# Down projection: the second block's weights loaded piece by piece, and its first row loads issued by GpSimd

## The chip, the cores and the metric

The kernel runs on one core of one Trainium2 chip. The metric is the device time of one execution in microseconds (us); lower is better. The time before is the median of three timed runs. The profile is one more execution, taken by the hardware profiler; its span runs from the first to the last instruction on the core. The engines are called PE (TensorE, the matmuls; its weight loads are shown apart as PEld), DVE (VectorE), ACT (ScalarE), POOL (GpSimd) and SP (SyncE, which here only issues DMAs).

## The reference

The block takes x (1024 tokens by 1024 channels, float32) and computes a dilated attention and a retention side by side, gates and merges them, projects, adds the input, and then runs a channel mixer. Only the end of that mixer is touched here:

```python
xn2 = rmsnorm(x, norm2_g[l])
x = x + jnp.square(jax.nn.relu(xn2 @ w_up[l])) @ w_down[l]
```

`w_up` is 1024 by 4096 and `w_down` is 4096 by 1024, so the hidden matrix h = relu(xn2 @ w_up) squared is 1024 by 4096.

## The kernel before, in words

**Numbers in two parts.** Every matmul operand is held as a high part and a low part (suffix h and l), made by `split` (lines 353 to 357): ACT copies the value into the high part (line 354) and DVE subtracts that from the value to get the low part (line 357). A product is then three matmuls, high by high, high by low and low by high. All matmuls are issued from line 257.

**Seven products for eight.** Large matmuls use Strassen's scheme with seven products called N1 to N7 on sums of quarter blocks. The up projection does so over 16 units (`strassen_order`), each a slice of 256 hidden columns. Its results are turned into the seven operands of the down projection, split (tile `hs`), and stored by SP to `h_d` in DRAM (line 1243).

**The down projection.** `h_d` is read back by rows. The down projection has 8 chunks c of 512 hidden columns and 4 row tiles t in each, 32 units u = 4c + t in all. One unit has seven products of six matmuls each. `load_rows(u)` (lines 1252 to 1260) reads the rows of one unit in two DMAs of 896 KB, `xh` and `xl`, both issued by SP at line 1259. There are three row buffers, taken in turn; they are the up projection's operand tiles (`OP7["N1"]`, `["N5"]`, `["N3"]`), so the first three row loads wait for the last up products that read them, and `load_rows(u + 3)` stands after unit u and waits for its last matmul. `down(u, name)` does one product. In the loop at the end, a pass for u does N6 and N5 of u, N1 of u + 1, N7 of u, N2 of u + 1, N3 and N4 of u; so a unit's rows are first read in the third product of the pass before its own. N1 and N2 of unit 0 are done among the last up products.

**What PE waits for inside a unit.** N1 goes into an accumulator of its own; ACT copies it, negated, into the accumulator of N6, N7 and N4 (line 1279, tile `ms`), and N2 is then added on top of N1, so N2 waits for that copy. The results of N2, N6, N5 and N4 are copied to `Y` by ACT in chunk 0 (line 1286) and added to `Y` by DVE afterwards (line 1288); N7 and N3 are added by DVE. N7 goes on top of N6 and so waits for N6's copy.

**The weights.** The class `Weights` keeps a list of loads and a list of steps for the whole kernel. A chunk of the down projection has four loads of 512 KB (`raw`, issued by SP at line 210, into four buffers used in turn) and seven steps in the order N1, N2, N3, N5, N7, N6, N4. A step splits one piece; those of N5, N7, N6 and N4 first take a sum or difference of two raw tiles on DVE (line 186). A step may go when the earlier piece in its buffer is done with (`free`, called after the last use) and all four loads of its chunk have been issued. `pump` issues all steps that may go, and after each as many loads as there are free raw buffers. Chunks with even c and with odd c have separate buffers; the odd set (`y1a` to `y1c`, 3, `w1a` to `w1c`) lies where up-projection tiles were, and comes free when the up projection is over.

**What sets the order.** Only PE runs in the order of the code (`manual_schedule`). On the other engines a planner orders the instructions: whichever it reckons ready goes first, and of several the one that stands earlier in the code. `tc.keep_in_program_order(i)` forbids it to put i ahead of the instruction that the code issued just before it on that engine; instructions that come later in the code may still pass it. Once the order is planned it is fixed: each engine, and SP with its DMAs, goes through its instructions strictly one after another, and an instruction whose wait is not over holds up all behind it.

Of the kernel before, what the change touches and what calls it, by code (L numbers as in the profile page):

```python
# [10 lines left out]
F = mybir.dt.float32  # L11
# [26 lines left out]
class Weights:  # L38
# [9 lines left out]
    RAW = 3  # L48
    A, B, C, D = (0, 1), (2, 3), 5, 4

    def __init__(self, nc, rawp, wp, split):
        self.nc, self.rawp, self.wp, self.split = nc, rawp, wp, split
        self.raw, self.used, self.next = [], set(), 0
        self.src, self.steps = [], []
        self.place, self.more, self.most = [], None, None
        self.last = {}
        self.units, self.done = {}, set()
        self.plain = self.taken = 0
        self.cycle, self.turn = tuple(range(self.WB)), 0

        self.places = {}

    def claim(self, buf, key):

# [105 lines left out]
    def add_chunks(self, tag, srcs, buffers):  # L170


        for c, quarters in enumerate(srcs):
            base = len(self.src)
            self.place += [(base + i) % (self.RAW + 1) for i in range(4)]
            self.src += quarters
            x00, x10, x11, x01 = range(base, base + 4)
            for name, r, other, op, ends in (
                    ("N1", x00, None, None, ()), ("N2", x10, None, None, ()), ("N3", x11, None, None, ()),
                    ("N5", x00, x01, OP.subtract, ()), ("N7", x01, x11, OP.subtract, (x01,)),  # L180
                    ("N6", x11, x00, OP.add, (x00,)), ("N4", x10, x11, OP.subtract, (x10, x11))):
                buf, key = buffers[c % 2][name], (tag, c, name)

                def step(r=r, other=other, op=op, ends=ends, buf=buf, key=key):
                    if other is not None:
                        self.nc.vector.tensor_tensor(self.raw[r], self.raw[r], self.raw[other], op=op)
                    h, l = self.buffer(buf)
                    self.split(h, l, self.raw[r])
                    self.units[key] = h, l
                    self.used.update(ends)  # L190

                self.steps.append((self.claim(buf, key), x01, step))
# [5 lines left out]

    def load(self):
        n = len(self.raw)  # L200
        if n >= len(self.src):
            return False
        b = self.place[n]
        if any(self.place[m] == b and m not in self.used for m in range(max(0, n - 16), n)):
            return False
        from_ = self.rawp if b < self.RAW else self.more if b == self.RAW else self.most
        if from_ is None:
            return False
        raw = from_.tile([P, UW], F, name=f"raw{b}", bufs=1)
        self.nc.sync.dma_start(raw[:, :self.src[n].shape[1]], self.src[n])  # L210
        self.raw.append(raw)
        return True
# [22 lines left out]

    def free(self, *ids):
        self.done.update(ids)
        self.pump()


class Pipe:
# [48 lines left out]
def strassen_order(units):  # L290


    order = [(0, "N1"), (1, "N1"), (0, "N2"), (1, "N2")]
    for j in range(units):
        late = j + 3 >= units
        order += [(j, "N6"), (j, "N5")] + ([] if late else [(j + 2, "N1")]) + [(j, "N7")]
        order += [(j, "N3")]
        order += [(j + 2, "N2")] if not late else [(units - 1, ("N1", "N2")[j + 3 - units])] if j + 1 < units else []
        order += [(j, "N4")]
    return order  # L300
# [3 lines left out]
def hybrid_block(ctx: ExitStack, tc: tile.TileContext, a: dict, out: bass.AP):  # L304
    nc = tc.nc
# [6 lines left out]
    rawp = pool(ctx, "rawp", 1)  # L312
    wp = pool(ctx, "wp", 1)
# [19 lines left out]
    h_d = dram.tile([FF // 512, 2, 4, P, 7, 2, P], F, name="h_d")  # L333
# [40 lines left out]
        return (slice(0, 512), slice(512, 1024))  # L374


    W = Weights(nc, rawp, wp, split)
    heads = [(slot, g) for slot in range(SLOTS) for g in (1, 2, 0)]
    for u in range(4):
        W.add(a["w_av"][u])  # L380
# [136 lines left out]
    with ExitStack() as ph:  # L517
# [96 lines left out]
        for n, t in enumerate(TILES):  # L614
# [4 lines left out]
            for k in range(KT):  # L619
                wh, wl = W[us[k // 2]]  # L620
                o = (k % 2) * 512
                xs = x01[t] if k < 4 and t >= 4 else [x[:, :, cut(t)] for x in XS[k // 4, t // 4]]
                terms.append((*(x[:, k % 4] for x in xs), wh[:, o:o + 512], wl[:, o:o + 512]))
            ends = {2 * i + 1: (lambda i=i: W.free(us[i])) for i in range(4)} if n == NT - 1 else None
            pipe.step(pm, terms, ends)
            c = px.tile([P, 512], F, name="c", bufs=1)
# [487 lines left out]
    with ExitStack() as ph:  # L1114
# [41 lines left out]
        def load_rows(n):  # L1156

            nb, t = order[n]
            ts = slice(t * P, (t + 1) * P)
            xt = pn.tile([P, 512], F, name="xr")  # L1160
            nc.sync.dma_start(xt, a["x"][ts, halves()[nb]])
            y0 = None
            if nb == 1:
                y0 = pn.tile([P, 512], F, name="y0")
                nc.sync.dma_start(y0, out[ts, :512])
            ahead.append((xt, y0))
# [34 lines left out]
    with ExitStack() as ph:  # L1201
# [50 lines left out]
        def load_rows(u):  # L1252

            if u < len(units):
                c, t = units[u]
                rows[u] = []
                for i, x in enumerate(OP7[("N1", "N5", "N3")[u % 3]]):
                    x = x.rearrange("p a b -> p (a b)")[:, :7 * 2 * P]
                    nc.sync.dma_start(x.bitcast(F), h_d[c, i, t].rearrange("p o k q -> p (o k q)"))
                    rows[u].append(x.rearrange("p (o k q) -> p o k q", o=7, k=2))  # L1260

        def down(u, name):
# [28 lines left out]
            if t == 3:  # L1291
                W.free(("dn", c, name))

        for j, name in strassen_order(NU):
            product("up", j, name, unit, OP7, temps, result)
            if j == NU - 1:
                if name == "N1":
                    load_rows(0)
                if name == "N2":
                    parts = [x.rearrange("p a b -> p (a b)") for x in OP7[name]]  # L1300
                    for i, part in enumerate("ab"):
                        W.places["n2" + part] = [x[:, 1024 * i:1024 * i + 1024] for x in parts]
                    W.free(("place", "n2"))
                if name == "N5":
                    load_rows(1)
                if name == "N7":
                    down(0, "N1")
                if name == "N3":
                    load_rows(2)
                    down(0, "N2")  # L1310
# [3 lines left out]
        Y.update({r: y1.tile([P, D], F, name=f"Y{r}") for t in (1, 3, 2) for r in (t, t + 4)})  # L1314
        for x in "abc":
            W.places["y1" + x] = [y1.tile([P, UW], R, name=f"y1{x}{i}") for i in "hl"]
        W.free(("place", "y1"))


    with ExitStack() as ph:  # L1320
        w1 = pool(ph, "w1", 1)
        for x in "abc":
            W.places["w1" + x] = [w1.tile([P, UW], R, name=f"w1{x}{i}") for i in "hl"]
        W.free(("place", "w1"))
        for u in range(len(units)):
            for name, later in (("N6", False), ("N5", False), ("N1", True), ("N7", False), ("N2", True),
                                ("N3", False), ("N4", False)):
                if u + later < len(units):
                    down(u + later, name)
            load_rows(u + 3)  # L1330
    sumst.close()


# [106 lines left out]
```

## Time and profile before

| | us |
|---|---|
| median of three runs | 2235.59 |
| lowest and highest of them | 2232.65, 2236.57 |
| the profiled execution's own time | 2232.95 |
| its span | 2231.2 |

| engine | busy us | share of the span |
|---|---|---|
| PE | 2182.3 | 98% |
| PEld | 1792.3 | 80% |
| DVE | 1435.4 | 64% |
| ACT | 1110.6 | 50% |
| POOL | 196.6 | 9% |

The down projection takes about the last 320 us of the span: its first row load is issued at 1870.74 us and its first matmul starts at 1898.69 us, while the last up products still run. In the timelines a row gives the start, the duration, the engine and line, the instruction's output and input, how many were merged, and in square brackets the idle time of the engine before it and what ended it. A stretch row gives its length and then for each engine its busy time and number of instructions, the clock granted to PE as a share, the mean busy share of the 16 DMA engines (overlapping packets can bring it over 1) and the GB/s moved.

### The profile page before, as it was taken

How to read it: one execution, taken by the hardware profiler on the slowest of the kernel's cores; microseconds unless marked ns; L12 is line 12 of the kernel's file. 1: busy time of each engine (PE TensorE's matmuls, PEld its weight loads, DVE VectorE, ACT ScalarE, POOL GpSimd, SP SyncE). 2: the span in 40 equal slices, each digit the busy share in tenths (PEclk: the TensorE clock that was granted, in tenths of full speed). 3: DMA queues.
4: the chain of work that ended last, by engine and by line, in shares of the span. 5: the costliest groups of instructions: out<-in, count | busy, mean ns of one | idle time of the engine just before them, and what ended most of it. 6: DMA issues, size and time to landing. Idle time of an engine off the chain costs nothing.

```text
span 2231.2 us, 28546 instructions
## 1 busy us (share of the span) xinstructions
PE 2182.3 (98%) x10064; PEld 1792.3 (80%) x10064; DVE 1435.4 (64%) x2543; ACT 1110.6 (50%) x1936; POOL 196.6 (9%) x184
## 2 busy tenths in 40 slices
PE   8999999999999999999999999999899999899998
PEld 6788788888788887888888788888788888688887
DVE  7766675455555556657767752453877778776863
ACT  6433444477844467745545532122577777522210
POOL 3314453000000000010000000000000000000002
PEclk9999999999999999999999999999999999999999
DMA  7344433544545555364333484554378889966658
GB/s 228 99 132 114 132 114 114 158 145 146 171 149 170 160 155 161 127 207 139 117 102 111 151 283 151 174 180 146 99 223 248 248 248 282 328 248 238 248 223 174
DMA packets 345664, 392.78 MB, mean 176 GB/s; under 512 B 34737, under 2 KB 270897, under 8 KB 345266
## 3 DMA queue, kind: packets, MB, share of 16 engines
q1 hardware_dynamic: 343026, 386.25, 55.0%
q0 software_dynamic: 2496, 4.72, 1.4%
q8 instruction: 79, 1.29, 0.2%
q14 instruction: 63, 0.52, 0.1%
HBM read 252.39 MB, written 138.51 MB: 175 GB/s over the span
## 4 chain that ended last, share of the span: by engine, by line
PE 81%; DVE 6%; ACT 4%; DMA 3%; issue 3%; POOL 2%; SPq 0%; POOLq 0%; ACTq 0%; DVEq 0%
PE mm L257 46%; PE ms L257 29%; DVE wl L357 1%; PE tr L792 1%; PE tr L811 1%; DMA xl<-h_d 1%; DMA raw<-in_w_att_q 1%; ACT wh L354 1%; PE tr L650 1%; DVE xl L357 1%; POOL x L555 1%; PE tr L804 1%; PE ms L934 1%; PE tr L990 1%; ACT xh L354 1%
## 5 line engine op out<-in xcount | busy, mean ns | idle before, releaser
L357 DVE TENSOR_TENSOR wl<-raw,wh 128x1024 fp32r<-128x1024 f32 (+1 forms) x292 | 332.3, 1143 | 175.2 <-ACT wh L354 173.4
L354 ACT ACTIVATE wh<-raw 128x1024 fp32r<-128x1024 f32 (+1 forms) x292 | 287.4, 988 | 253.1 <-PE ms L257 122.1
L257 PE MATMUL mm<-xh,wh 128*128 128x512 f32 x896 | 346.8, 410 | 1.9 <-ACT wh L354 1.2
L257 PE MATMUL mm<-xl,wh 128*128 128x512 f32 x896 | 329.5, 391 | 1.7 <-DVE xl L357 1.7
L257 PE MATMUL mm<-xh,wl 128*128 128x512 f32 x768 | 301.2, 392 | 0.5 <-DVE wl L357 0.5
L257 PE MATMUL mm<-wh,xh 128*128 128x512 f32 x736 | 296.3, 403 | 0.8 <-ACT ms L1279 0.6
L257 PE MATMUL mm<-wh,xl 128*128 128x512 f32 x736 | 288.6, 392 | 4.5 <-DMA xl<-h_d 4.5
L257 PE MATMUL mm<-wl,xh 128*128 128x512 f32 x736 | 287.6, 391 | 0.0
L257 PE MATMUL ms<-xh,wh 128*128 128x512 f32 x544 | 225.6, 415 | 1.8 <-DVE St L981 1.2
L257 PE MATMUL ms<-xh,wl 128*128 128x512 f32 x544 | 212.9, 391 | 0.0
L257 PE MATMUL ms<-xl,wh 128*128 128x512 f32 x544 | 212.4, 390 | 0.0
L257 PEld LDWEIGHTS mm<-xh,wh 128*128 128x128 f32 x896 | 169.2, 189 | 34.4 <-ACT wh L354 1.6
L257 PEld LDWEIGHTS mm<-xl,wh 128*128 128x128 f32 x896 | 169.3, 189 | 31.8 <-DVE xl L357 2.1
L257 PEld LDWEIGHTS mm<-xh,wl 128*128 128x128 f32 x768 | 144.6, 188 | 32.4 <-DVE wl L357 1.0
L257 PEld LDWEIGHTS mm<-wh,xl 128*128 128x128 f32 x736 | 138.4, 188 | 35.1 <-DMA xl<-h_d 5.4
L257 PEld LDWEIGHTS mm<-wh,xh 128*128 128x128 f32 x736 | 138.7, 188 | 27.2 <-ACT ms L1279 1.0
L257 PEld LDWEIGHTS mm<-wl,xh 128*128 128x128 f32 x736 | 138.8, 189 | 25.8
L257 PE MATMUL ms<-wh,xh 128*128 128x512 f32 x336 | 137.0, 408 | 6.0 <-DVE c L705 3.4
L257 PE MATMUL ms<-wh,xl 128*128 128x512 f32 x336 | 133.3, 397 | 2.5 <-DVE xl L357 2.5
L257 PE MATMUL ms<-wl,xh 128*128 128x512 f32 x336 | 132.5, 394 | 0.8 <-DVE wl L357 0.8
L257 PEld LDWEIGHTS ms<-xh,wh 128*128 128x128 f32 x544 | 102.5, 188 | 21.9 <-DVE St L981 1.6
L257 PEld LDWEIGHTS ms<-xh,wl 128*128 128x128 f32 x544 | 102.1, 188 | 22.0
(284 smaller groups left out, 3816.4 us busy)
## 6 DMA issues: line engine op xcount, KB each, us to landing
h_d<-hs SPq DMA_DIRECT2D x112, 512.0 KB, 4.2
xh<-h_d SPq DMA_DIRECT2D x32, 896.0 KB, 6.1
xl<-h_d SPq DMA_DIRECT2D x32, 896.0 KB, 7.3
raw<-in_w_att_q SPq DMA_DIRECT2D x48, 512.0 KB, 4.2
raw<-in_w_up SPq DMA_DIRECT2D x32, 512.0 KB, 3.7
raw<-in_w_down SPq DMA_DIRECT2D x32, 512.0 KB, 5.2
qk_d<-T SPq DMA_DIRECT2D x48, 256.0 KB, 3.5
raw<-in_w_gate_q SPq DMA_DIRECT2D x16, 512.0 KB, 4.4
```

Of the source, the lines that this page charges most:

```text
L257: self.nc.tensor.matmul(ps, x, y, start=start, stop=stop, skip_group_check=not first)
L354: hi = nc.scalar.activation(dst_h, src, AF.Copy)
L357: nc.vector.tensor_tensor(dst_l, src, dst_h.bitcast(F), op=OP.subtract)
L555: nc.gpsimd.tensor_tensor(x[v], x[v], x[u], op=op)
L650: nc.tensor.transpose(pt[:, i, :], c[:, i * P:(i + 1) * P], ident)
L792: nc.tensor.matmul(sp[:, :w], q[:, e * P:(e + 1) * P], k[:, k0 * P:k0 * P + w], start=True, stop=True)
L804: nc.tensor.transpose(tb[:, j * P:(j + 1) * P], st["p"][:, j * P:(j + 1) * P], ident)
L811: nc.tensor.matmul(po[:, :DH], st["t"][:, j * P:(j + 1) * P], v[:, k0 + j, :], start=(j == 0), stop=(j == nk - 1))
L934: nc.tensor.matmul(sp[:, :P], kT[:, f], qT[:, f], start=(f == 0), stop=(f == 1))
L990: nc.tensor.transpose(pt[:, f, :], it["o"][:, f * P:(f + 1) * P], ident)
```

## The change

Two things are changed around the beginning of the down projection.

First, the weights of chunk 1 (the second block). A `limit` stops the raw loads of chunk 1 from being issued in the code before the down loop, and `eager = False` stops `free` from pumping from the end of the up projection on. In passes 1 to 3 of the loop, after every product, `ease` raises the limit by one load, up to the end of chunk 1's four, and lets one step go. The first four calls thus allow the four loads, and the fourth to the tenth issue the seven pieces, N1 first and N4 last. The high parts of these pieces, and the sums on DVE that precede four of them, are pinned behind what the code issued before them. After pass 3 the limit is lifted, `eager` is set again and `pump` issues all that may go, which is chunk 2's loads and pieces. No instruction on DVE, ACT or PE is added or left out.

Second, the row loads of units 0 to 7 (16 DMAs) are issued by GpSimd instead of SP.

```diff
+        self.limit, self.eager = None, True
+        self.bases = {}
...
-            base = len(self.src)
+            base = self.bases[tag, c] = len(self.src)
...
-                def step(r=r, other=other, op=op, ends=ends, buf=buf, key=key):
+                def step(r=r, other=other, op=op, ends=ends, buf=buf, key=key, pinned=c == 1):
                     if other is not None:
-                        self.nc.vector.tensor_tensor(self.raw[r], self.raw[r], self.raw[other], op=op)
+                        d = self.nc.vector.tensor_tensor(self.raw[r], self.raw[r], self.raw[other], op=op)
+                        if pinned:
+                            self.tc.keep_in_program_order(d)
                     h, l = self.buffer(buf)
-                    self.split(h, l, self.raw[r])
+                    self.split(h, l, self.raw[r], pinned)
...
     def load(self):
         n = len(self.raw)
-        if n >= len(self.src):
+        if n >= (len(self.src) if self.limit is None else self.limit):
             return False
...
     def free(self, *ids):
         self.done.update(ids)
-        self.pump()
+        if self.eager:
+            self.pump()
+
+    def ease(self, last):
+
+        if self.limit is not None:
+            self.limit = min(self.limit + 1, last)
+        self.pump(1)
...
-                    nc.sync.dma_start(x.bitcast(F), h_d[c, i, t].rearrange("p o k q -> p (o k q)"))
+                    (nc.gpsimd if u < 8 else nc.sync).dma_start(x.bitcast(F), h_d[c, i, t].rearrange("p o k q -> p (o k q)"))
...
+        W.limit = W.bases["dn", 1]
         for j, name in strassen_order(NU):
...
+        W.eager = False
         W.free(("place", "y1"))
...
                 if u + later < len(units):
                     down(u + later, name)
+                if 0 < u < 4:
+                    W.ease(W.bases["dn", 2])
             load_rows(u + 3)
+            if u == 3:
+                W.limit, W.eager = None, True
+                W.pump()
```

More of the change, by code (lines that the diff above doesn't have):

```diff
@@ L49, with __init__ @@
     A, B, C, D = (0, 1), (2, 3), 5, 4
-    def __init__(self, nc, rawp, wp, split):
-        self.nc, self.rawp, self.wp, self.split = nc, rawp, wp, split
+    def __init__(self, tc, rawp, wp, split):
+        self.tc, self.nc, self.rawp, self.wp, self.split = tc, tc.nc, rawp, wp, split
         self.raw, self.used, self.next = [], set(), 0
@@ L374, in halves @@
         return (slice(0, 512), slice(512, 1024))
-    W = Weights(nc, rawp, wp, split)
+    W = Weights(tc, rawp, wp, split)
     heads = [(slot, g) for slot in range(SLOTS) for g in (1, 2, 0)]
```

## The prediction

> **What bounds the kernel now.** I read the page first, then the stretches around the start of the down projection, then what PE waited for there, and last the queue that the change touches. The page's span, its busy row for PE and the granted clock in forty slices:
>
> ```profile
> span 2231.2 us, 28546 instructions
> PE 2182.3 (98%) x10064; PEld 1792.3 (80%) x10064; DVE 1435.4 (64%) x2543; ACT 1110.6 (50%) x1936; POOL 196.6 (9%) x184
> ...
> PEclk9999999999999999999999999999999999999999
> ```
>
> PE is busy for 98% of the span, so only time in which PE stands still or runs at a lower clock can be won. Stretches of ten us show where that is:
>
> ```profile
> core 0: us, PE busy (x) PEld busy (x) DVE busy (x) ACT busy (x) POOL busy (x), PEclk, DMA share, GB/s
> 1910.00:1920.00 10.00, 9.01 (x40) 7.14 (x39) 8.64 (x13) 7.82 (x14) 0.00 (x0) 1.00 1.08 330
> 1920.00:1930.00 10.00, 6.89 (x31) 5.39 (x30) 0.69 (x1) 2.83 (x5) 0.00 (x0) 1.00 1.00 324
> 1930.00:1940.00 10.00, 8.38 (x31) 6.23 (x30) 9.41 (x9) 6.68 (x9) 0.00 (x0) 0.86 0.76 310
> 1940.00:1950.00 10.00, 8.11 (x34) 6.29 (x33) 8.86 (x9) 6.01 (x8) 0.00 (x0) 0.97 0.93 321
> 1950.00:1960.00 10.00, 9.53 (x35) 7.72 (x36) 5.94 (x8) 3.59 (x5) 0.00 (x0) 0.83 0.55 207
> 1970.00:1980.00 10.00, 10.00 (x46) 8.28 (x45) 4.50 (x7) 0.58 (x1) 0.00 (x0) 1.00 0.63 225
> ```
>
> A stretch at full pace shows some 45 matmuls; between 1920 and 1960 the four show 31, 31, 34 and 35, and the granted clock falls to 0.86 and 0.83. After 1970 nothing is left to win. The waits of the PE weight loads from 1850 us on name the cause:
>
> ```profile
> PEld mm L257 <- DMA xl<-h_d: 8.2, 3, 3.5
> PEld mm L257 <- ACT ms L1279: 1.6, 2, 1.0
> PEld ms L257 <- ACT Y L1286: 1.4, 1, 1.4
> ```
>
> Three waits for row loads make 8.2 us; ACT's copies cost 3.0. The rows of these waits, with two neighbours:
>
> ```profile
> 1921.27 0.19 PEld L257 LDWEIGHTS mm<-wl,xh 128*128 128x128 f32 x1
> 1924.99 0.19 PEld L257 LDWEIGHTS mm<-wh,xl 128*128 128x128 f32 x1 [3.53 <-DMA xl<-h_d]
> ...
> 1934.54 0.19 PEld L257 LDWEIGHTS mm<-wh,xh 128*128 128x128 f32 x1 [0.60 <-issue]
> 1936.67 0.19 PEld L257 LDWEIGHTS mm<-wh,xl 128*128 128x128 f32 x1 [1.84 <-DMA xl<-h_d]
> 1938.09 0.33 PEld L257 LDWEIGHTS ms<-xl,xh 128*128 128x128 f32 x1
> 1938.51 0.33 PEld L257 LDWEIGHTS ms<-xh,xl 128*128 128x128 f32 x1
> ...
> 1950.47 0.19 PEld L257 LDWEIGHTS mm<-y1ah,xl 128*128 128x128 f32 x1 [2.78 <-DMA xl<-h_d]
> ```
>
> They are the first uses of `xl` of units 2, 3 and 4, each in the N1 product. What PE does after the second is slow as well: one matmul every 0.42 us (1938.09 to 1938.51). Why the loads came late is in SP's queue:
>
> ```profile
> 1907.96 1.14 SPq L210 DMA_DIRECT2D raw<-in_w_down  x1
> 1909.19 0.53 SPq L1259 DMA_DIRECT2D xh<-h_d  x1
> 1912.67 3.74 SPq L1243 DMA_DIRECT2D h_d<-hs  x3
> 1916.46 1.09 SPq L1259 DMA_DIRECT2D xl<-h_d  x1
> 1917.64 2.12 SPq L1243 DMA_DIRECT2D h_d<-hs  x2
> 1919.81 6.09 SPq L210 DMA_DIRECT2D raw<-in_w_down  x3
> 1926.00 0.38 SPq L1259 DMA_DIRECT2D xh<-h_d  x1
> ...
> 1931.44 0.32 SPq L1259 DMA_DIRECT2D xh<-h_d  x1
> 1938.39 5.43 SPq L210 DMA_DIRECT2D raw<-in_w_down  x4
> 1943.92 0.38 SPq L1259 DMA_DIRECT2D xl<-h_d  x1
> ...
> 1978.04 0.32 SPq L1259 DMA_DIRECT2D xh<-h_d  x1
> ...
> 1987.56 0.32 SPq L1259 DMA_DIRECT2D xh<-h_d  x1
> ```
>
> Unit 2's `xl` goes out 7.3 us after its `xh` (1909.19 to 1916.46), with three stores of the up projection between them. Unit 3's rows stand behind three weight loads that hold SP for 6.09 us, and unit 4's `xl` goes out 12.5 us after its `xh` (1931.44 to 1943.92), behind four weight loads. The code issues the two side by side, so the planner put the others between. The last two rows are the pace without waits: one unit every 9.52 us, or 0.227 us for each of its 42 matmuls, 1.36 us a product.
>
> **The change part by part.** *The waits that go.* The three lose 3.5, 0.6 + 1.8 and 2.8 us, 8.7 together. Less the pitch that runs on when PE restarts (about 0.1 for each of the four pauses) that is 8.3. The slow spells cost, at 0.42 against 0.227 us, some 0.2 us for each matmul. The deficit of the clock is (1 - 0.86) x 10 = 1.4 us in one stretch, 0.3 + 1.7 in the next two, 3.4 in all, of which the matmuls feel what PE was not waiting for; I take 3.0. So the late rows cost 11.3 us.
>
> *Row loads by GpSimd.* Sixteen issues leave SP and go to POOL. The price of an issue there, and its cover, are in these rows (`out` is stored by POOL, 256 KB each; the first row is the one at 2186.89):
>
> ```profile
> 2186.89 0.97 POOL L1290 DMA_DIRECT2D out<-Y  x1 [591.07 <-DVE Y L1288]
> ...
> L1290 POOL DMA_DIRECT2D out<-Y x16: 856/874/966, 2186.9 to 2225.0; - x16
> ...
> DMA to landing us min/median/max: 3.9/5.0/10.2
> ```
>
> POOL did nothing for the 591 us before 2186.89, so 16 x 0.87 = 14 us lie beside everything, and there is nothing in POOL's queue to stand behind. In it each pair waits for PE to be done with a row buffer, and behind it only later pairs wait. What counts is the latency. By the row 1921.27, N1 of unit 2 begins at 1921.04; it is the third product of pass 1, so pass 1 begins and unit 0 ends 2 x 1.36 us earlier, at 1918.3. The first use of `xl` of unit u + 3 comes 9.52 + 2.72 + 0.45 = 12.7 us after unit u ends. Against this stand two issues, 1.7 us, and the landing. How long rows took on SP's queue between 1900 and 1960, and over the whole kernel's `xl`:
>
> ```profile
> xl<-h_d SPq DMA_DIRECT2D x5, 896.0 KB, 8.5
> ...
> DMA to landing us min/median/max: 6.2/7.3/10.8
> ```
>
> 1.7 + 8.5 = 10.2 us fits in 12.7; 1.7 + 10.8 = 12.5 just fits. How long 896 KB takes from POOL no row shows: below, as on SP; above, `out`'s median of 5.0 us scaled by the size (3.5 times) gives 17.5 us, and a late unit. I take SP's 8.5, since `out` adds to DRAM and the rows are a plain read like SP's, and price the wait at zero.
>
> The Trainium skill, page "DMA: Bandwidth & Descriptors", section "Issuing engines are not separate DMA queues", speaks against this half: all issuers share the same 16 DMA engines, and a second issuer only saves sequencer time, usually small beside the transfer. By it alone the gain would be a few issue times, under 2 us, and the sum about 2234. The SP rows of 7.3 and 12.5 us between two issues side by side decide otherwise: what is saved is standing in line.
>
> *Weights of chunk 1.* The same four loads, seven splits and four sums, later. The limit only holds back where the code issues the loads; the planner may still put them before stores that wait, so I expect at most the one at 1907.96 to move, behind the last store at about 1920, next to the three that go there already. They are due at N1 of unit 4: 1921.04 + 2 x 9.52 = 1940.1. Splits and landings before:
>
> ```profile
> 1931.01 1.06 ACT L354 ACTIVATE y1ch<-raw 128x1024 fp32r<-128x1024 f32 x1 [0.51 <-DMA raw<-in_w_down]
> ...
> L354 ACT ACTIVATE wh<-raw x8: 1047/1056/1062, 1904.6 to 1962.7; 128x1024 fp32r<-128x1024 f32 x8
> L186 DVE TENSOR_TENSOR raw<-raw,raw x10: 1214/1218/1226, 1902.8 to 1961.5; 128x1024 f32<-128x1024 f32 x10
> ```
>
> The third load landed at 1931.0, so the fourth at about 1932. N5, N7 and N6 each take a sum of 1.22 and a high part of 1.06 us, one after the other some 6.9 us, until 1939; the last is due in pass 4, which begins at 1918.3 + 3 x 9.52 = 1946.9. The weights themselves are in time. The cost is the wait that the pins add: N6's high part stands, in the order of the code, ahead of the `ms` copy of N1 of unit 3, and N2 of unit 3 (due 1930.6 + 2.7 = 1933.3) waits for that copy. If the planner leaves the copy (0.58 us) behind, N2 begins near 1939.4, 6.1 us late; if it passes the copy ahead, nothing is lost. Between 0 and 6.1 I take 2.0, nearer to the lower end, since the planner may pass every copy ahead of a piece whose sum is not ready.
>
> *Chunk 2.* Its pieces go out after pass 3, at about 1947; N1 of unit 8 is due at 1940.1 + 4 x 9.52 = 1978. In these 31 us the loads land (by the 8.5 above) and DVE does seven low parts and four sums of 1.22 us, 13.4 us: free. Without that cover each us late would cost one.
>
> **Sum.** Against the profiled execution's 2232.95: -11.3 for the late rows and their slow spells, +2.0 for ACT, rest nothing: 2223.6. The median stands 2.6 above that execution, so the sum is 2226.3 on the median's scale, and I forecast 2226.
>
> **The rivals.**
> *The pieces hold ACT.* The copy stays behind, 6.1 us and a slow spell of 1.5 take the place of the row waits: 2235.6 - 11.3 + 7.6 = 2232. For it: ACT already waited for a raw load at 1931.01. Against: the planner's freedom.
> *The DMA engines are the bound.* Their share is 1.00 or more until 1930 while they move 324 GB/s, so a row pair brought forward pushes stores and weights back, 0.9 MB by 2.8 us, and PE waits for those. Then only the third wait and its spell, at shares of 0.93 and 0.55, can go: 2.8 + 1.6 = 4.4, time 2231. Against: in the stretch of the second wait the share was 0.76.
> *Slower: rows from POOL land late.* With 17.5 us for `xl`, 1.7 + 17.5 is 6.5 us more than 12.7. Three row buffers in turn mean that a late unit delays the two after it too, so the wait returns every third unit, at 3 and at 6: 13.0, and two slow spells of 1.6: 2235.6 - 11.3 + 16.2 = 2240. It decides from 11.3 - 3.2 = 8.1 over two waits, a landing of about 15 us. Against: `out`'s longest landing is 10.2.
> *Better.* ACT's present 3.0 us mostly go too, as DVE and ACT lose a piece near 1915, and the pins cost nothing: 2235.6 - 11.3 - 2.4 = 2222.
> *The change does not do what it says.* The planner issues the loads as before; then rows of unit 3 share the DMA engines with three weight loads, 1.5 MB or 4.7 us at 324 GB/s, half of it late by at most 2: 2228.
>
> **How the numbers follow.** The forecast 0.50, better 0.13, loads not moved 0.07, pieces 0.12, DMA engines 0.10, slower 0.08. About 0.2%, 4.5 us, can be told from no change, so faster begins below 2231.1: the first three and half of the DMA case, 0.75; same 0.17; slower 0.08. The range begins at 2219 (the better case on the profiled execution's scale) and reaches to 2235, past the two cases that give most back; the slower case and some of the same ones stay out.
>
> **What would show it.** In the changed profile the rows of `xl` should stand on POOL, in pairs 0.9 us apart from about 1919, with no gap beside them on PE; PEclk should be 1.00 from 1920 to 1960, and each of these stretches should show 44 or more matmuls. The ACT step is wrong if waits for the `ms` or `Y` copies between 1925 and 1945 exceed 2 us. POOL rows landing above 12 us, or PE still waiting for `xl`, would make the forecast wrong.

## The result: slower by 0.35%, where faster was forecast

The changed kernel takes 2243.11 us (median of ten runs, 2237.51 to 2246.36). The kernel before, timed beside it on the same chip, takes 2233.55 (2231.75 to 2238.44). The ratio is 1.0035, with a 95% interval of 1.0027 to 1.0043: 9.6 us lost, as much as was forecast to be won.

The profiled execution of the changed kernel, 2246.36 us, is the slowest of its ten. Both kernels issue the same 10064 matmuls in the same order, so the start of each can be compared in the two traces. The 8500th, at 1853 us, where the two kernels still do the same work, comes 4.5 us later in the changed one. This lag arises before anything that was changed and isn't explained by it; all lags below are counted from that matmul on. One row of the page after, with each engine's busy time, its share of the span and its number of instructions; the lines have moved (raw loads L214, sums of raw tiles L188, matmuls L268, splits L365 and L368, stores of `hs` L1254, row loads L1270, copies L1290 and L1297, additions to `Y` L1299):

```profile
PE 2186.7 (97%) x10064; PEld 1797.2 (80%) x10064; DVE 1433.8 (64%) x2543; ACT 1109.1 (49%) x1936; POOL 205.5 (9%) x200
```

**What went as forecast.** The rows are in time. POOL's timeline after, at the loads of units 2 and 3:

```profile
1912.73 0.53 POOL L1270 DMA_DIRECT2D xl<-h_d  x1 [5.67 <-PE mm L268]
1913.34 0.53 POOL L1270 DMA_DIRECT2D xh<-h_d  x1
1935.95 0.54 POOL L1270 DMA_DIRECT2D xh<-h_d  x1 [22.08 <-PE ms L268]
1936.58 0.53 POOL L1270 DMA_DIRECT2D xl<-h_d  x1
```

The number in square brackets is POOL's idle time before, and PE ends it: each pair goes out side by side, 0.6 us apart, when PE is done with the buffer. The view of DMA issues gives 8.1 us from issue to landing for the eight `xl` (median; 8.5 was taken). And among the waits of the PE weight loads from 1850 us on (total, times, longest, us) there is no `xl` any more:

```profile
PEld ms L268 <- ACT Y L1297: 7.5, 1, 7.5
PEld ms L268 <- DVE Y L1299: 6.1, 7, 4.2
PEld mm L268 <- ACT u L443: 3.5, 1, 3.5
PEld mm L268 <- DVE Y L1299: 1.0, 1, 1.0
PEld mm L268 <- ACT ms L1290: 0.8, 1, 0.8
```

But 18.9 us of other waits stand there. The stretches after show where PE stood and where its clock fell:

```profile
core 0: us, PE busy (x) PEld busy (x) DVE busy (x) ACT busy (x) POOL busy (x), PEclk, DMA share, GB/s
1890.00:1900.00 10.00, 10.00 (x34) 7.95 (x34) 7.26 (x9) 7.25 (x12) 0.00 (x0) 0.74 0.84 237
...
1920.00:1930.00 10.00, 2.91 (x9) 2.06 (x8) 1.99 (x3) 4.24 (x8) 0.00 (x0) 0.80 1.08 380
1930.00:1940.00 10.00, 10.00 (x39) 8.10 (x39) 2.82 (x5) 3.04 (x6) 1.06 (x2) 0.86 1.04 317
...
1970.00:1980.00 10.00, 6.47 (x19) 4.55 (x20) 10.00 (x12) 3.18 (x3) 0.00 (x0) 0.83 0.61 200
```

Against 45 or 46 matmuls at full pace there are 34, 9, 39 and 19. The lag behind the kernel before, by matmul (its time in the kernel before in the head, from the traces):

| lag, us, at the matmul of | 1886 | 1915 | 1954 | 1973 | 1991 |
|---|---|---|---|---|---|
| changed kernel | 5.2 | 12.5 | 1.5 | 8.3 | 8.3 |

So there are two losses before 1915, then 11.0 us won back where the three row waits stood before, then 6.8 lost again.

**The first two losses are stores that come late.** `hs` has four buffers. ACT may write the next one only when the store of an old one has landed, and ACT goes strictly in order. Its timeline after, all three waits for a store:

```profile
1887.95 0.63 ACT L365 ACTIVATE hs<-q 128x512 fp32r<-128x512 f32 x1 [6.41 <-DMA h_d<-hs]
1922.12 0.63 ACT L365 ACTIVATE hs<-u 128x512 fp32r<-128x512 f32 x1 [4.52 <-DMA h_d<-hs]
1926.24 0.63 ACT L365 ACTIVATE hs<-q 128x512 fp32r<-128x512 f32 x1 [3.49 <-DMA h_d<-hs]
...
1927.26 0.59 ACT L1297 ACTIVATE Y<-ms 128x512 f32<-128x512 f32 x1
```

Behind the first stands the `u` copy for which PE waits 3.5 us; behind the others the `Y` copy at 1927.26 for which it waits 7.5. These waits are 14.4 us together; before they were 6.1. In the chain of waits the stores that release ACT are these:

```profile
1878.68 9.19 DMA h_d<-hs
...
1912.90 13.26 DMA h_d<-hs
```

In the chain before, the longest store between 1870 and 1900 took this long (of all stores issued from 1865 to 1930 us, on the chain or off it, the longest took 8.8 us to land before and 14.3 after):

```profile
1874.19 6.79 DMA h_d<-hs
```

Who held them up stands in the view of the DMA queues (packets, MB, share of the 16 engines; `software_dynamic` is POOL's queue, `hardware_dynamic` SP's). From 1880 to 1883 us, while the store issued at 1878.68 was still to land, the rows of unit 0, which POOL had issued at 1875.29 and 1875.91, had the engines almost alone:

```profile
q0 software_dynamic: 158, 1.02, 97.9%
q1 hardware_dynamic: 6, 0.00, 0.3%
```

From 1918 to 1922, while the store issued at 1912.90 was still to land:

```profile
q0 software_dynamic: 179, 1.15, 68.3%
q1 hardware_dynamic: 203, 0.52, 32.6%
```

And from 1924 to 1930, when POOL's queue had one packet left:

```profile
q1 hardware_dynamic: 3386, 2.16, 112.2%
```

POOL's rows go in packets of 7168 B, the stores in packets of 512 B and the weight loads beside them in packets of 4096 B. In the first stretch SP's queue moved next to nothing. In the second it got 0.52 MB in 4 us, 0.13 MB per us, and nearly all of that was 119 packets of weight loads, so the stores got almost nothing. When the rows were through, SP's queue moved 0.36 MB per us. The Trainium skill says this of the DMA engines (page "DMA: Bandwidth & Descriptors", section "Queues, rings and completion order"): each takes turns between the queues it has work for, a packet at a time. The trace agrees with turns one for one only from 1918 to 1922, 179 to 203; from 1880 to 1883 it is 158 to 6, and over 1910 to 1924 it is 575 to 1650. So the trace shows that the rows took most of the engines' time in these stretches, but not by what rule the two queues share it.

**SP's queue** after shows a second thing:

```profile
1908.82 2.71 SPq L214 DMA_DIRECT2D raw<-in_w_down  x2
1912.90 8.38 SPq L1254 DMA_DIRECT2D h_d<-hs  x2
1921.37 3.32 SPq L214 DMA_DIRECT2D raw<-in_w_down  x1
```

Three of chunk 1's four loads stand among the last stores, where before only one did (1907.96). With the rows gone from SP, the planner put them there in spite of the limit. The first two stand ahead of the store of 1912.90, and theirs are the packets of 4096 B above.

**The order on ACT** has a part in the second loss. In the kernel before, the `Y` copy that PE waits for stood ahead of the last pieces of `hs`:

```profile
1912.35 0.58 ACT L1286 ACTIVATE Y<-ms 128x512 f32<-128x512 f32 x1
...
1913.88 1.15 ACT L354 ACTIVATE hs<-q 128x512 fp32r<-128x512 f32 x2
```

There 109 of the 112 `hs` pieces stood ahead of this copy; after, the planner put 110 ahead of it, and the one more is that of 1926.24 with its wait of 3.49 us. Behind the copy, it would have let the copy go some 4 us earlier (an estimate from these rows: the wait and about 0.5 us for the piece). So the 7.5 us are late stores and a new order together, and no run of the changed kernel parts the two.

**The third loss** is at chunk 2. Its weights landed between 1957 and 1966 us, and in the stretch from 1970 DVE was busy for 10.00 of 10 us, with pieces and with the additions to `Y` that stand behind them:

```profile
1972.95 0.19 PEld L268 LDWEIGHTS ms<-w1ah,xh 128*128 128x128 f32 x1 [4.21 <-DVE Y L1299]
```

### The profile page after: what moved, and what is told of

It reads as the page before. It is cut to its first block, busy times and chain, and to the rows that moved or that the text cites. A ratio compares the mean times of both kernels' runs of the same rounds, so it can differ in the third digit from the quotient of the medians.

```text
span 2244.6 us, 28555 instructions
## 1 busy us (share of the span) xinstructions
PE 2186.7 (97%) x10064; PEld 1797.2 (80%) x10064; DVE 1433.8 (64%) x2543; ACT 1109.1 (49%) x1936; POOL 205.5 (9%) x200
## 4 chain that ended last, share of the span: by engine, by line
PE 82%; DVE 7%; ACT 4%; DMA 4%; issue 2%; POOL 1%; SPq 0%; POOLq 0%; ACTq 0%; DVEq 0%
PE mm L268 46%; PE ms L268 30%; DVE wl L368 2%; PE tr L803 1%; PE tr L822 1%; DVE xl L368 1%; DMA h_d<-hs 1%; ACT wh L365 1%; PE tr L661 1%; DMA raw<-in_w_att_q 1%; PE ms L945 1%; PE tr L815 1%; DVE raw L155 1%; POOL x L566 1%; PE tr L1001 1%
## 5 line engine op out<-in xcount | busy, mean ns | idle before, releaser
L368 DVE TENSOR_TENSOR wl<-raw,wh 128x1024 fp32r<-128x1024 f32 (+1 forms) x292 | 331.4, 1141 | 179.7 <-ACT wh L365 177.8
L365 ACT ACTIVATE wh<-raw 128x1024 fp32r<-128x1024 f32 (+1 forms) x292 | 287.2, 987 | 257.1 <-PE ms L268 128.5
L268 PE MATMUL mm<-xh,wh 128*128 128x512 f32 x896 | 347.8, 411 | 4.5 <-ACT u L443 3.0
L268 PE MATMUL mm<-xl,wh 128*128 128x512 f32 x896 | 330.3, 392 | 1.7 <-DVE xl L368 1.7
L268 PE MATMUL mm<-xh,wl 128*128 128x512 f32 x768 | 301.9, 393 | 0.5 <-DVE wl L368 0.5
L268 PE MATMUL mm<-wh,xh 128*128 128x512 f32 x736 | 296.8, 403 | 0.0
L268 PE MATMUL mm<-wh,xl 128*128 128x512 f32 x736 | 288.6, 392 | 0.0
L268 PE MATMUL mm<-wl,xh 128*128 128x512 f32 x736 | 288.0, 391 | 0.0
L268 PE MATMUL ms<-xh,wh 128*128 128x512 f32 x544 | 226.1, 416 | 1.8 <-DVE St L992 1.2
L268 PE MATMUL ms<-xl,wh 128*128 128x512 f32 x544 | 212.8, 391 | 0.7 <-DVE xl L368 0.7
L268 PE MATMUL ms<-xh,wl 128*128 128x512 f32 x544 | 213.1, 392 | 0.0
L268 PEld LDWEIGHTS mm<-xh,wh 128*128 128x128 f32 x896 | 169.8, 190 | 37.2 <-ACT u L443 3.5
L268 PEld LDWEIGHTS mm<-xl,wh 128*128 128x128 f32 x896 | 169.7, 189 | 31.7 <-DVE xl L368 2.1
L268 PEld LDWEIGHTS mm<-xh,wl 128*128 128x128 f32 x768 | 145.0, 189 | 32.4 <-DVE wl L368 1.0
L268 PEld LDWEIGHTS mm<-wh,xl 128*128 128x128 f32 x736 | 138.6, 188 | 29.9
L268 PEld LDWEIGHTS mm<-wl,xh 128*128 128x128 f32 x736 | 139.2, 189 | 25.9
L268 PEld LDWEIGHTS mm<-wh,xh 128*128 128x128 f32 x736 | 138.9, 189 | 25.8
L268 PE MATMUL ms<-wh,xh 128*128 128x512 f32 x336 | 138.3, 412 | 6.8 <-DVE c L716 4.3
L268 PE MATMUL ms<-wh,xl 128*128 128x512 f32 x336 | 134.0, 399 | 2.5 <-DVE xl L368 2.5
L268 PE MATMUL ms<-wl,xh 128*128 128x512 f32 x336 | 133.8, 398 | 0.5 <-DVE wl L368 0.5
L268 PEld LDWEIGHTS ms<-xh,wh 128*128 128x128 f32 x544 | 102.6, 189 | 22.5 <-DVE St L992 1.6
L268 PEld LDWEIGHTS ms<-xh,wl 128*128 128x128 f32 x544 | 102.2, 188 | 21.9
```

Source lines behind the costliest of these rows:

```text
L268: self.nc.tensor.matmul(ps, x, y, start=start, stop=stop, skip_group_check=not first)
L365: hi = nc.scalar.activation(dst_h, src, AF.Copy)
L368: nc.vector.tensor_tensor(dst_l, src, dst_h.bitcast(F), op=OP.subtract)
```

## The experiments

The change has two halves, so the first four kernels take them apart. All kernels were run beside the kernel before, whose medians were 2233.1 to 2234.8. The lags are those of their profiled executions, counted as above. The lag of one execution and the difference of the medians can be up to 4 us apart (for the second row -4.9 by the last lag and -8.7 by the medians): the times decide which kernel is faster, and the lags say where.

| kernel | median us | ratio, 95% interval | lag at 1886 | 1915 | 1954 | 1973 | 1991 |
|---|---|---|---|---|---|---|---|
| all eight units' rows by GpSimd, weights as before | 2244.60 | 1.0043 (1.0031 to 1.0056) | 3.8 | 15.1 | 10.8 | 10.5 | 10.5 |
| weights as changed, rows by SP | 2226.08 | 0.9957 (0.9943 to 0.9970) | -0.9 | -0.8 | -10.1 | -6.7 | -4.9 |
| rows of units 3 to 7 by GpSimd, weights as before | 2233.31 | 0.9995 (0.9986 to 1.0003) | -0.4 | -0.4 | 0.2 | -0.5 | -0.5 |
| weights as changed, rows of 3 to 7 by GpSimd | 2238.21 | 1.0017 (1.0008 to 1.0026) | -0.9 | -1.4 | -7.7 | 2.0 | 2.0 |
| weights as changed, rows of 0 to 2 by GpSimd | 2242.50 | 1.0036 (1.0022 to 1.0049) | 3.1 | 11.7 | 2.0 | 7.2 | 10.2 |
| all rows by GpSimd, units 0 to 2 cut to 256 KB, weights as before | 2234.73 | 0.9999 (0.9988 to 1.0010) | -0.6 | 5.6 | -2.0 | -2.3 | -2.3 |
| weights as changed, rows of 3 to 7 by GpSimd, cut to 256 KB | 2235.11 | 1.0009 (1.0001 to 1.0018) | -0.9 | -0.2 | -7.0 | 0.3 | 0.3 |
| weights as changed, rows by SP, chunk 2 eased too | 2229.19 | 0.9981 (0.9972 to 0.9989) | -0.7 | -1.8 | -10.9 | -7.9 | -6.1 |
| weights as changed without pins, rows by SP | 2232.89 | 0.9994 (0.9984 to 1.0005) | -0.9 | -0.9 | -10.4 | -9.4 | -2.2 |
| limit alone, rows by SP | 2238.68 | 1.0016 (1.0005 to 1.0028) | -0.4 | -0.4 | -7.6 | 6.7 | 6.7 |
| weights as changed, rows of 0 to 2 by GpSimd in 512 B pieces | 2258.68 | 1.0107 (1.0092 to 1.0122) | -0.9 | 16.2 | 19.4 | 24.0 | 25.7 |
| changed kernel, rows by GpSimd in 512 B pieces | 2306.36 | 1.0317 (1.0299 to 1.0336) | -0.9 | 15.6 | 36.1 | 57.0 | 70.0 |

### Each half alone

The kernel before with the second half only:

```diff
-                    nc.sync.dma_start(x.bitcast(F), ...)
+                    (nc.gpsimd if u < 8 else nc.sync).dma_start(x.bitcast(F), ...)
```

> The kernel before with only the row loads of units 0 to 7 moved to GpSimd; the weights as before. Theory A (crowding): the row pairs of units 0 to 2, now early and in a queue of their own, take DMA time from the up projection's stores; hs buffers come free late, ACT stands, PE with it, at two places (after's waits of 3.5 us on u and 7.5 us on Y). Against that the 11 us of row waits go. In the trace of after both together are +1.5 us up to about 1960, so A expects 0 to +4 us against before, with both ACT waits present and the DVE wait of 4.2 us near 1973 absent. Theory B (the weights part does the harm: its pins and later loads reorder ACT and DVE): the row waits go and no new ACT waits come, -8 to -11 us, about 2224.

Its waits of the PE weight loads and of ACT from 1850 us on:

```profile
PEld ms L257 <- ACT Y L1286: 11.6, 1, 11.6
...
PEld mm L257 <- ACT u L432: 3.4, 1, 3.4
...
ACT hs L354 <- DMA h_d<-hs: 14.2, 4, 6.3
```

This half alone costs 0.43%, and shows the changed kernel's first two losses. It is 9.8 us slower than the kernel before, where the worse theory had 4 at most. Next the changed kernel with all rows back on SP:

```diff
-                    (nc.gpsimd if u < 8 else nc.sync).dma_start(x.bitcast(F), ...)
+                    nc.sync.dma_start(x.bitcast(F), ...)
```

> The change without its second half: chunk 1's weights eased in, row loads on SP as before. A: no ACT wait on stores beyond those of before (0.6 us); a DVE wait behind chunk 2's seven pieces, issued at once after pass 3, of about 5 us with its slow spell (+6.8 us in the trace of after); unit 2's row wait stays (3.5 us), those of units 3 and 4 may shrink because fewer weight loads stand before them, by up to 7.9 us: in all -1 to +7 us against before. B: +8 us or more, with ACT waits on stores as in after.

It is faster than both kernels, 8.7 us against the kernel before, which neither theory had. The waits of its PE weight loads:

```profile
PEld ms L268 <- DVE Y L1299: 4.2, 7, 2.6
PEld mm L268 <- ACT ms L1290: 2.6, 2, 1.9
PEld mm L268 <- DMA xl<-h_d: 2.0, 1, 2.0
```

Its SP queue:

```profile
1922.01 4.07 SPq L1270 DMA_DIRECT2D xh<-h_d  x1
1926.17 0.45 SPq L1270 DMA_DIRECT2D xl<-h_d  x1
1926.67 1.88 SPq L214 DMA_DIRECT2D raw<-in_w_down  x4
1932.49 0.33 SPq L1270 DMA_DIRECT2D xh<-h_d  x1
1932.91 0.38 SPq L1270 DMA_DIRECT2D xl<-h_d  x1
```

Here the limit does what it says: chunk 1's four loads go out after the last store, unit 3's rows stand ahead of them, and unit 4's pair is side by side, where before 12.5 us lay between. One of the three row waits, 2.0 us, is left. So the standing in line, which I meant to remove by a second queue, goes away by holding the weight loads back.

### Which rows do the harm

```diff
+                    (nc.gpsimd if 3 <= u < 8 else nc.sync).dma_start(x.bitcast(F), ...)
```

> The kernel before with only the row loads of units 3 to 7 issued by GpSimd; units 0 to 2 stay on SP behind the stores, and the weights are as before. A: the up projection's stores are left alone, the waits of units 3 and 4 with their slow spells go (0.6 + 1.8 + 1.6 and 2.7 + 1.6, about 8 us), unit 2's 3.5 us stays: about -8 us, 2226. B agrees for this kernel. If rows from GpSimd are themselves slow, the waits of units 3 to 7 stay and the time is that of before.

No change, where both theories had -8 us: the row waits of units 3 and 4 are gone, and waits for copies take their place. ACT stands at a piece whose weights come late:

```profile
1935.63 1.06 ACT L354 ACTIVATE y1bh<-raw 128x1024 fp32r<-128x1024 f32 x1 [5.03 <-DMA raw<-in_w_down]
```

Before, ACT split the same piece at 1929.45 us without a wait. The same line in the changed kernel:

> The change with GpSimd issuing only the row loads of units 3 to 7. A: -8 us for the rows, +6.8 us for chunk 2's burst on DVE: -3 to +1 us against before, so 8 to 11 us faster than the change itself. B: the harm stays, +5 us or more against before.

It is 3.4 us slower than the kernel before, between the two theories. Moving five units' rows costs 12 us against the faster kernel (2238.21 to 2226.08). The lags put most of it between 1954 and 1973, at the additions to `Y`. The longest of these waits of the PE weight loads:

```profile
1970.48 0.29 PEld L268 LDWEIGHTS ms<-w1ch,xh 128*128 128x128 f32 x1 [3.89 <-DVE Y L1299]
```

The other group, units 0 to 2:

> The weights as in the changed kernel; rows of units 0 to 2 (six loads) by GpSimd, all others by SP. The changed kernel takes 2243.1 us, with rows 3 to 7 alone on GpSimd 2238.2, with all rows on SP 2226.1. Theory A (each group of rows takes the DMA engines' bytes from whatever SP moves in the same stretch: units 0 to 2 from the up projection's stores, units 3 to 7 from the weight loads of chunks 1 and 2): rows 0 to 2 cost by themselves, through ACT waits for stores of the operand tile of 10 us and more and PE waits for the u and Y copies; 2232 to 2238 us. Rival B (nothing is wrong with rows 0 to 2 on GpSimd; the harm is all in units 3 to 7, where the planner brings weight loads forward when SP's queue has fewer rows): within 2224 to 2229 us, ACT waits for stores as with all rows on SP, 4.5 us.

Its waits of PE and ACT:

```profile
PEld ms L268 <- ACT Y L1297: 8.9, 1, 8.9
...
ACT hs L365 <- DMA h_d<-hs: 16.0, 4, 5.7
```

These six loads alone bring the whole time of the changed kernel, 2242.50 against 2243.11, more than either theory had. The two groups don't add up (16 and 12 us over the faster kernel, 17 together); why, no run shows.

### Bytes or order

A row load on another queue changes two things: the bytes that meet on the DMA engines, and the order that the planner writes for all engines. The first is mostly taken away by loading two of the seven operands of units 0 to 2 (the other five keep old data, so this kernel's output is not the reference's). SP, POOL, ACT, DVE and PE have the same instructions in the same order as with full rows, by their traces:

```diff
-                    (nc.gpsimd if u < 8 else nc.sync).dma_start(x.bitcast(F), h_d[c, i, t].rearrange(...))
+                    m = 2 if u < 3 else 7
+                    (nc.gpsimd if u < 8 else nc.sync).dma_start(x[:, :m * 2 * P].bitcast(F), h_d[c, i, t, :, :m].rearrange(...))
```

> The kernel with only the row loads of units 0 to 7 moved to GpSimd (9.8 us slower than before), in which the rows of units 0 to 2 are cut: they load 2 of the 7 operands, 256 KB instead of 896 KB a DMA, so the output is not the reference's. Same queues, same number of DMAs, same early issue; only the bytes that share the DMA engines with the stores shrink. Crowding: ACT's waits on stores fall from 14.2 us to 6 or less, the PE waits on u (3.4) and Y (11.6) shrink to about 1 us each, and the time falls by 10 us or more against the uncut kernel, to 2225 to 2234. If GpSimd's issue or its own queue were to blame whatever the bytes, both waits stay and the time is about 2244.

9.9 us less than with full rows. How long the stores issued from 1865 to 1935 us took to land, with full rows and then with cut ones:

```profile
DMA to landing us min/median/max: 3.2/5.8/13.8
...
DMA to landing us min/median/max: 3.2/5.5/7.9
```

The waits of PE and ACT with cut rows:

```profile
PEld ms L257 <- ACT Y L1287: 6.4, 1, 6.4
...
ACT hs L354 <- DMA h_d<-hs: 3.7, 2, 2.1
```

ACT's waits for stores fall from 14.2 to 3.7 us and the wait for `u` is gone: these were the rows' bytes, since nothing else differs. A wait of 6.4 us for the `Y` copy stays, with little waiting for stores behind it. In ACT's timeline the copy, at 1918.77 us, stands behind the high parts of `y1a` (1915.59) and `y1c` (1917.29): the order that the planner chose. Before, neither stood ahead of that copy. Of the 11.3 us lost between 1886 and 1915 with full rows, 6.2 stay by the lags, and the cut kernel is no faster than the kernel before: what it wins by having its rows in time (7.6 us by 1954), this order takes again for the most part. The same cut for units 3 to 7, with the weights as changed:

> The weights as in the changed kernel, rows of units 3 to 7 by GpSimd, but these loads bring only two of the seven operands (256 KB in place of 896 KB; the other five hold old data, so the output is not the reference's; the number of instructions is the same). With full rows: 2238.2 us, 12 us above the kernel with all rows on SP. Theory A (bytes: the rows take the DMA engines from chunk 1's and chunk 2's weight loads, whose pieces then hold DVE ahead of the Y adds): most of the 12 us goes, 2226 to 2230 us, PE waits for the Y adds on DVE fall from 7.4 and 1.4 us to under 5. Rival B (the planner's changed order on SP, DVE and ACT, which does not depend on how many bytes a row load has on the chip): 2235 to 2239 us, with the same waits for the Y adds.

Only 3.1 of the 12 us go, and the waits for the `Y` additions stay (6.6 and 1.5 us in total, 7.4 and 1.4 with full rows). So for these rows the bytes that were cut are the smaller part. What is left is put down to the order by exclusion; no run changes the order alone. In both kernels all twelve loads of chunks 1 to 3 stand in one block of SP's queue with no row between them, and on DVE pieces stand ahead of the additions.

### What the weights' half is made of

Chunk 2's loads and pieces in passes 4 to 6, one by one and pinned, rows by SP:

```diff
-                def step(..., pinned=c == 1):
+                def step(..., pinned=c in (1, 2)):
...
+                if 3 < u < 7:
+                    W.ease(W.bases["dn", 3])
...
-            if u == 3:
+            if u == 6:
```

> The weights part with rows on SP (8.7 us faster than before), and chunk 2's pieces eased and pinned too: the limit now rises again in passes 4 to 6, one load and one piece per product, and is lifted after pass 6. Theory of the burst (seven unpinned pieces issued at once after pass 3 stand before the sums into Y on DVE): the DVE wait of 2.6 us with its slow spell goes, 3 to 5 us faster still, about 2222. If the burst is not the cause, the time stays at 2226; if easing only moves the burst to chunk 3, the wait shows up some 40 us later.

Not faster than without by the times (2229.19 to 2226.08), though 1.2 us ahead by the last lag; the longest wait for a `Y` addition is 2.3 us (2.6 without), and 4.8 us are lost from 1954 on as against 5.2. Handing chunk 2 out one piece at a time doesn't remove that loss. Without the pins, rows by SP:

```diff
-                def step(..., pinned=c == 1):
+                def step(..., pinned=False):
```

> The weights part with rows on SP, without the pins on chunk 1's high parts and sums. If the order of the loads in SP's queue makes the gain, the time stays within 2 us of 2226. If the pins make it, the gain of 8.7 us is mostly lost, 2231 or more, with ACT held by pieces ahead of the ms and Y copies.

The row waits go as before (-10.4 at 1954), but 7.2 us are lost between 1973 and 1991, where one wait stands. So most of the gain goes with the pins, but the wait is for DVE, where ACT was expected to be held:

```profile
PEld mm L268 <- DVE Y L1299: 4.7, 1, 4.7
```

And the limit alone, lifted after pass 0, with no handing out and no pins, rows by SP:

```diff
-                if 0 < u < 4:
-                    W.ease(W.bases["dn", 2])
...
-            if u == 3:
+            if u == 0:
```

> Of the weights part only the holding back: chunk 1's loads are held until pass 0 is over and then everything is issued at once, no pins, rows on SP. If it is enough that unit 3's rows stand before chunk 1's loads on SP, the row waits of units 2 to 4 shrink as in the weights part: 5 to 9 us faster than before, 2226 to 2230. If the one piece per product matters, unit 4's rows still stand behind loads and pieces hold ACT: within 3 us of before.

Slower than before, which neither case had, with its loss from 1954 on:

```profile
PEld ms L268 <- DVE Y L1299: 10.0, 6, 8.6
```

Holding the loads back wins 7.6 to 10.9 us by 1954 in all of them, though PE still waits for rows for 1.5 to 5.1 us; what it costs at chunk 2 depends on the order of pieces and additions on DVE: 5.2 us with pins, 8.2 without, 14.3 with everything let go at once.

### Smaller packets

If the queues take turns by packets, smaller packets for the rows should leave more for the stores. The rows go in two DMAs each, one for each k:

```diff
+                        for k in range(2):
+                            nc.gpsimd.dma_start(x.bitcast(F).rearrange("p (o k q) -> p k o q", o=7, k=2)[:, :, k], h_d[c, i, t, :, :, k])
```

> The weights as in the changed kernel and rows of units 0 to 2 by GpSimd, as in the kernel that took 2242.5 us; each row load is now issued as two DMAs, one for each k, so the same 896 KB go in pieces of 512 B in place of 7168 B. SP, ACT, DVE and PE have the same instructions in the same order. Theory A (the 16 DMA engines take turns between the two queues packet by packet, so that packets of 7168 B on POOL's queue leave little to the stores' packets of 512 B): stores and rows now share the bytes, ACT waits for stores of the operand tile fall from 16.0 us to under 8, and the PE waits for the u and Y copies from 11.6 to under 6; 2230 to 2237 us, unless the rows themselves come late. Rival B (the bytes that must be moved before the stores decide, whatever the packets): within 2240 to 2245 us, with the same waits.

The waits of PE and ACT:

```profile
PEld mm L268 <- DMA xh<-h_d: 13.8, 2, 7.4
PEld mm L268 <- DMA xl<-h_d: 10.8, 2, 6.4
...
ACT hs L365 <- DMA h_d<-hs: 4.4, 2, 3.5
```

POOL's timeline, with two half loads:

```profile
1928.37 0.94 POOL L1272 DMA_DIRECT2D xl<-h_d  x1 [5.98 <-issue]
1933.20 0.94 POOL L1272 DMA_DIRECT2D xh<-h_d  x1 [3.89 <-issue]
```

ACT's waits for stores fall from 16.0 to 4.4 us and those of PE for the `Y` copy vanish, as the theory of turns has it; but the time rises to 2258.68, because the rows come late. POOL issues one load only every five to eight us, in seven of the eleven pauses without waiting for anything that the profile shows. The packets on its queue were of 4096 B, not 512, and the rate fell at the same time, so this run shows the stores in time when the rows come slowly; it doesn't part the turns from the rate. With all eight units:

> The changed kernel, with the row loads of units 0 to 7 by GpSimd in pieces of 512 B (two DMAs for each load) in place of 7168 B; the order of the other engines is the same. The changed kernel takes 2243.1 us. Theory A: the waits for stores, for the u copy (3.5) and for the Y copy (7.5) shrink to under half; the wait of 4.2 us for the Y add on DVE behind chunk 2's pieces, which hangs on the planned order, stays; 2231 to 2238 us. Rival B: within 2241 to 2246 us, with the same waits.

PE waits for `xl` twelve times, 52.7 us in all: both theories' times are missed for the same reason.

## Why the prediction was wrong

**What bounds the kernel: right.** Three row waits and their slow spells were priced at 11.3 us. In the changed kernel the lag falls by 11.0 between 1915 and 1954.

**Row loads by GpSimd, priced at zero: the step that failed.** "What counts is the latency", I wrote, and the latency was right: 0.6 us between the two issues and 8.1 to land, inside the 12.7 of slack. What I left out is whom the rows displace. On SP they had waited behind the stores; on their own queue they met the stores on engines whose share I had quoted as 1.08 and 1.00 (in the kernel before it is 0.99 to 1.01 from 1870 to 1890 too, where the first loss stands). Stores took 9.2 and 13.3 us, ACT stood behind them, and PE lost 5.2 us by 1886 and 7.3 more by 1915. In the kernel with this half alone, cutting the bytes in the same order took the waits for stores from 14.2 to 3.7 us and 9.9 us off the time. I also left out that the planner would order ACT anew once the rows are gone from SP: with the bytes cut, 6.4 us of waiting for the `Y` copy stay. How the 7.3 us divide between bytes and order in the changed kernel stays open. I looked for the cost of the move at the place that it was to help, between 1920 and 1960; both losses begin before it, with the rows of units 0 to 2.

**The rival "the DMA engines are the bound"** had the mechanism but not the sign. It priced 0.9 MB at 2.8 us once, as if a store pushed back only cost its own delay, and I set it aside for a share of 0.76 in a stretch where no store was left. The victims were the stores ahead of it, and while the rows ran they had two thirds of the engines' time and more (68.3% and 97.9% in the two stretches).

**The Trainium skill's section on issuing engines** ("DMA: Bandwidth & Descriptors", "Issuing engines are not separate DMA queues"), which I overruled by the standing in line, says in its first half that all issuers' transfers share the 16 engines and interleave. The queue rows of 1918 to 1922 show both queues on the same engines. By that section of the Trainium skill the half could win little; alone it measured +0.43%.

**Weights of chunk 1, +2.0 in bounds of 0 to 6.1: about right.** With rows on SP, the one wait for an `ms` copy that counts is 1.9 us, behind a piece whose sum is late, as I argued, though one unit later. That the limit holds back "at most the one at 1907.96" was right only with the rows on SP; with them on POOL two more loads moved forward, the case "the change does not do what it says", to which I gave 0.07. What these loads add to the stores' lateness stays open: from 1918 to 1922 most of what SP's queue moved was theirs, but when the rows were cut, three loads still went out before 1910, ahead of the last stores, and ACT's waits for stores fell all the same.

**Chunk 2, "free": wrong.** The 31 us cover the loads and the sum of DVE's work, but not its place: pieces and additions to `Y` share DVE's one order, and some additions come late. 6.8 us in the changed kernel, 5.2 in the one with rows on SP. The cover was reckoned for the pieces, not for what stands behind them. How to avoid it stays open; easing chunk 2 did not.

**Sum.** Not -11.3 + 2.0, but 5.2 + 7.3 - 11.0 + 6.8 = +8.3 in the profiled execution. The forecast of 2226 is what the weights' half gives alone, 2226.08, though by another route than I argued: SP's order, not a second queue, freed the rows. That the two numbers meet is chance. The slower rival (rows from POOL land late) was wrong in its reason: no row of the changed kernel was late.

## What to carry to other kernels

A transfer that stands in line is also a transfer that lets others pass: before moving it to a queue of its own, ask whose bytes it will take in that stretch, what waits for those (here a buffer that comes free, an engine in strict order, a copy), and whether holding back the traffic ahead of it does the same without a second queue. Work that is put off has to be priced at the new place for what stands behind it on its engine, not only for its own due time. And two halves of a change should be timed apart: here one was worth -0.43% and the other +0.43%, and the better kernel was the first alone.

## What the runs showed of the hardware

Two queues shared the 16 DMA engines unevenly: POOL's rows, in packets of 7168 B, had 97.9% of their time from 1880 to 1883 us, with 158 packets to 6 of SP's, and 68.3% from 1918 to 1922, with 179 to 203. A row load of 896 KB was issued by POOL in 0.53 us, less than the 0.87 of the stores that I had scaled from; the same bytes in runs of 512 B took 0.94 us for each half load and came only every five to eight us. And issuing on SP isn't always cheap: two stores held it for 8.38 us (1912.90), where two had taken 2.12 before (1917.64).
